# Eight instead of sixteen taps of a 31-tap depthwise convolution on TensorE, the rest on VectorE

## The chip, the cores and the metric

The kernel runs on one core of a Trainium2 chip. Its engines work beside each other, each through a queue of its own that is served in order: TensorE (PE, its weight loads PEld), VectorE (DVE), ScalarE (ACT), GpSimd (POOL) and SyncE (SP), which here only issues DMA transfers. The metric is the time of one execution on the device in microseconds (us). The kernel before takes 2657.86 us (median of 3 runs, 2657.32 to 2660.58).

## The reference

One inference step of a two-layer diffusion backbone over 128 prompt tokens and 512 latent tokens, 640 in all, with 1024 channels in float32. Each layer is a gated feed-forward part, a mixer, and a second feed-forward part, each with a residual. The mixer of the second (odd) layer is the one that matters here:

```python
def gmlp_conv_mixer(h, w_in, v_ln_g, v_ln_b, sp_w, sp_b, dw_w, dw_b, cn_g, cn_b, w_out):
    u, v, ga, gg = jnp.split(h @ w_in, [D_C, 2 * D_C, 2 * D_C + D_D], axis=-1)
    u = jax.nn.gelu(u)
    v = layer_norm(jax.nn.gelu(v), v_ln_g, v_ln_b)
    vc = v.reshape(b, L // MLP_CHUNK, MLP_CHUNK, N_HEADS_C, HEAD_DIM_C)
    sv = jnp.einsum('hts,bcshd->bcthd', sp_w, vc) + sp_b.T[None, None, :, :, None]
    y_c = u * sv.reshape(b, L, D_C)
    glu = ga * jax.nn.sigmoid(gg)
    y_d = jax.nn.silu(layer_norm(depthwise_conv_centred(glu, dw_w, dw_b), cn_g, cn_b))
    return jnp.concatenate([y_c, y_d], axis=-1) @ w_out
```

`depthwise_conv_centred(glu, dw_w, dw_b)` convolves each of the 1024 channels of `glu` along the tokens with 31 taps of its own (`CONV_D = 31`), the 128 and the 512 tokens apart, and adds a bias.

## The kernel before

**Layout.** Activations are stored with channels on the 128 partitions and tokens along the free dimension: eight blocks of 128 channels by 640 tokens. The tokens are worked on in two halves of 320, A and B. A dense product in float32 is made of three products of rounded parts (`mm3`: high weight times high input, high times low, low times high), so that each weight block arrives by DMA (`wr`, issued by SP, L206), is cast to its high part on ACT (`wh`, L216), and has its low part taken on DVE (`wl`, L217). The prefetch runs two weight units ahead, and four raw buffers hold what has landed and is not yet split.

**The odd mixer, in the order of TensorE.** First the `ga` and `gg` products for the eight channel blocks j (each 48 matmuls for half A, then 48 for half B); their gated product goes into a padded tile `pads[j]` of 685 columns (L1301). Then the `v` products (in two passes q of four weight units each, 512 columns wide, L1333 to L1335). Then the `u` products for eight blocks, each followed, two blocks late, by the spatial product `sv` (L1353), whose result is combined on DVE (L1358, L1360) into `yc[j]`. The eight `yc` are split into high and low parts (L366 on ACT, L367 on DVE). Then come 16 tasks `ooc` (the output product over the `yc`), with the layer norm of the convolution woven in, and last the output product over the normalized convolution, `ood`.

**The convolution of a block j** has 31 taps. `PE_TAPS` of them run on TensorE, as matmuls on 32 x 32 diagonal blocks: `rep_next` copies the padded tile four times by 16 DMAs on the SP queue, each copy shifted by one more token (`rep`, L1254), and builds the diagonal weights on DVE (`diag`, L1257); `conv` then runs four matmuls for each group of four taps and each of two column halves (L1269), and ACT brings the sum with the bias into a tile `cacc` of 655 columns (L1272). The other taps are a chain on DVE: each step multiplies the padded tile, shifted by one token, with the tap's weight and adds it to `cacc` in place (L1276); the last tap writes the result `co[j]` (L1281, two pieces). So a step of one chain needs the step before it, while steps of two blocks' chains do not need each other.

```python
ng = PE_TAPS // 4
dg = ph.tile([P, ng * 4, 32], F32, tag="s", name=nm("diag"))
...
for m in range(PE_TAPS // 4):
    for q in range(4):
        TE.matmul(ps[32 * q:32 * q + 32, :q1 - q0], lhsT=dg[:, 4 * m + q, :],
                  rhs=R[q][:, 4 * m + q0:4 * m + q1], ...)
S.activation(out=ac[:, q0:q1], in_=ps[:, :q1 - q0], func=AF.Identity, bias=cvc("dw_b", j))
rep_next()
with tc.high_priority(offset=-CONV_LATE):
    for i in range(PE_TAPS, CONV_D - 1):
        V.scalar_tensor_tensor(out=ac, in0=pad[:, i:i + 655], ..., in1=ac, ...)
```

**What sets the order.** TensorE's order is written out by hand: block j's convolution runs at the slots `CONV_AT = (1, 2, 3, 4, 5, 7, 9, 11)`, five between the A and B halves of the gate products and three between the units of the `v` products. `LN_STEPS` puts the sums of the layer norm over all eight `co[j]` (`ln_sum`, L1389, 32 matmul records) directly before the first `ooc` task. The other engines' order is fixed ahead of the run by a planner: on each engine it takes, among the instructions that it holds ready at that moment of its own plan, the one of highest priority, and an instruction that is not ready in the plan is passed over. The taps on DVE have the lowest priority (`CONV_LATE = 3000`), so all else that is ready goes first. On the chip each engine then keeps that order. Padded tiles, `rep`, `diag`, `cacc`, `co`, `yc` and some others share one pool of 21 buffers (`OB`).

Of the kernel before, what the change touches and what calls it, by code (L numbers as in the profile page):

```python
# [30 lines left out]
RB = 4  # L31
NSTD = 3
TAP_EARLY = 400
PE_TAPS = 16
RW = 655 + PE_TAPS - 4
REPS = 1
OB = 21
# [34 lines left out]
def build(tc, ap):  # L72
# [3 lines left out]
    with ctx:  # L76
# [11 lines left out]
        def nm(p):  # L88
            uid[0] += 1
            return f"{p}_{uid[0]}"  # L90
# [49 lines left out]
        def psum(cols=512):  # L140
            return pspool.tile([P, cols], F32, tag="ps", name=nm("ps"))
# [13 lines left out]
        def cvc(name, i):  # L155
            o = CV[name] + i
            return cv[:, o:o + 1]
# [1062 lines left out]
        def odd(prev):  # L1220
# [26 lines left out]
            def rep_next():  # L1247
# [4 lines left out]
                for r in range(4):  # L1252
                    for q in range(4):
                        nc.sync.dma_start(out=R[q][32 * r:32 * r + 32, :], in_=pads[j][32 * q:32 * q + 32, r:r + RW])  # L1254
                ng = PE_TAPS // 4
                dg = ph.tile([P, ng * 4, 32], F32, tag="s", name=nm("diag"))
# [4 lines left out]
            def conv(j):  # L1261
# [3 lines left out]
                for q0, q1 in ((0, 328), (328, 655)):  # L1265
                    ps = psum()
# [3 lines that stand above are left out]
                                      rhs=R[q][:, 4 * m + q0:4 * m + q1],  # L1270
                                      start=(m == 0), stop=(m == PE_TAPS // 4 - 1))
# [4 lines that stand above are left out]
                        V.scalar_tensor_tensor(out=ac, in0=pad[:, i:i + 655], scalar=cvc("dw_w", i * 8 + j), in1=ac,  # L1276
# [285 lines left out]
```

## Time and profile before

| What | Value |
|---|---|
| Median of 3 runs | 2657.86 us |
| The profiled execution, its own time | 2652.47 us |
| Its span in the trace | 2650.7 us |
| Mean granted TensorE clock over the span | 0.987 of full speed |
| The odd mixer's first convolution on PE starts at | 1842.1 us in the span |
| ScalarE (ACT) busy from 1842.70 to 2064.00 | 59.30 us |

Times in the trace count from the span's start. An engine's busy time says how long it worked, not whether anything waited for it. TensorE's matmuls are pipelined: a record's duration is longer than the step from one start to the next, so the rate is read from starts, or from the pieces of the chain that ended last. Idle time of an engine is followed by the engine and line that released it. Profile and timed runs are different executions.

### The profile page before, as it was taken

How to read it: one execution, taken by the hardware profiler on the slowest of the kernel's cores; microseconds unless marked ns; L12 is line 12 of the kernel's file. 1: busy time of each engine (PE TensorE's matmuls, PEld its weight loads, DVE VectorE, ACT ScalarE, POOL GpSimd, SP SyncE). 2: the span in 40 equal slices, each digit the busy share in tenths (PEclk: the TensorE clock that was granted, in tenths of full speed). 3: DMA queues.
4: the chain of work that ended last, by engine and by line, in shares of the span. 5: the costliest groups of instructions: out<-in, count | busy, mean ns of one | idle time of the engine just before them, and what ended most of it. 6: DMA issues, size and time to landing. Idle time of an engine off the chain costs nothing. (4 is left out here: it accounts for less than half of the span.)

```text
span 2650.7 us, 43732 instructions
## 1 busy us (share of the span) xinstructions
PE 2525.2 (95%) x17229; PEld 2434.1 (92%) x17229; DVE 1936.4 (73%) x3265; ACT 1245.7 (47%) x2316; POOL 154.4 (6%) x255
## 2 busy tenths in 40 slices
PE   7899999899999999999999999989999999999997
PEld 5899999889989999999999999989879998999997
DVE  6778878589986977677597777855985749554465
ACT  4444445458863644445354444543223536444552
POOL 0011110000000010101001011000000000101100
PEclk9999999999999999999999999999999999999999
DMA  7487876222112376767238687724431123656641
GB/s 283 122 225 205 214 220 168 76 70 64 48 53 88 104 207 182 204 187 196 80 116 212 182 227 210 198 93 123 133 112 64 56 72 112 175 143 147 157 120 58
DMA packets 140078, 378.09 MB, mean 143 GB/s; under 512 B 17504, under 2 KB 24160, under 8 KB 139360
## 3 DMA queue, kind: packets, MB, share of 16 engines
q1 hardware_dynamic: 111568, 296.33, 34.4%
q0 software_dynamic: 24768, 71.31, 15.2%
q10 hardware_dynamic: 3536, 7.66, 0.9%
q8 instruction: 135, 2.21, 0.3%
q14 instruction: 71, 0.58, 0.1%
HBM read 329.17 MB, written 3.67 MB: 126 GB/s over the span
## 5 line engine op out<-in xcount | busy, mean ns | idle before, releaser
L217 DVE TENSOR_TENSOR wl<-wr,wh 128x1024 fp32r<-128x1024 f32 (+3 forms) x393 | 390.6, 997 | 294.4 <-ACT wh L216 107.3
L216 ACT CAST wh<-wr 128x1024 fp32r<-128x1024 f32 (+3 forms) x393 | 339.7, 868 | 376.8 <-DMA wr<-in_wd 119.2
L384 PE MATMUL ps<-h,wl 128*128 128x320 f32 x1408 | 436.9, 310 | 9.8 <-DVE wl L217 9.8
L382 PE MATMUL ps<-h,wh 128*128 128x320 f32 x1408 | 437.0, 310 | 6.3 <-ACT h L366 6.3
L383 PE MATMUL ps<-h,wh 128*128 128x320 f32 x1408 | 436.1, 310 | 3.1 <-DVE h L367 3.1
L745 PE MATMUL ps<-quad,wh 128*128 128x320 f32 x1824 | 406.8, 311 | 3.8 <-ACT tmp L727 3.8
L745 PE MATMUL ps<-th,wh 128*128 128x320 f32 x1216 | 382.3, 314 | 28.4 <-ACT tmp L727 22.9
L745 PE MATMUL ps<-th,wl 128*128 128x320 f32 x1216 | 380.0, 313 | 3.6 <-DVE wl L217 3.6
L745 PE MATMUL ps<-tl,wh 128*128 128x320 f32 x1216 | 379.3, 312 | 0.0
L313 DVE CUSTOM_DVE_ANT_0 junk<-wm,crow,cv 128x1024 bf16<-128x1024 f32 x256 | 327.6, 1280 | 3.3 <-DMA wm<-in_wm 0.7
L382 PE MATMUL ps<-pair,wh 128*128 128x320 f32 (+1 forms) x976 | 309.3, 317 | 8.4 <-ACT pair L375 5.8
L745 PEld LDWEIGHTS ps<-quad,wh 128*128 128x128 f32 x1824 | 307.7, 189 | 4.6 <-ACT tmp L727 4.5
L383 PE MATMUL ps<-pair,wh 128*128 128x320 f32 (+1 forms) x976 | 304.0, 312 | 2.1 <-DVE pair L377 2.1
L384 PE MATMUL ps<-pair,wl 128*128 128x320 f32 (+1 forms) x976 | 303.7, 311 | 0.0
L745 PE MATMUL ps<-quad,wl 128*128 128x320 f32 x912 | 283.5, 311 | 4.9 <-DVE wl L217 4.9
L384 PEld LDWEIGHTS ps<-h,wl 128*128 128x128 f32 x1408 | 264.6, 188 | 14.0 <-DVE wl L217 14.0
L382 PEld LDWEIGHTS ps<-h,wh 128*128 128x128 f32 x1408 | 264.6, 188 | 8.3 <-ACT h L366 8.0
L383 PEld LDWEIGHTS ps<-h,wh 128*128 128x128 f32 x1408 | 264.6, 188 | 5.2 <-DVE h L367 4.7
L745 PEld LDWEIGHTS ps<-th,wh 128*128 128x128 f32 x1216 | 231.4, 190 | 35.4 <-ACT tmp L727 28.4
L217 DVE TENSOR_TENSOR wl<-ws,wh 128x1024 fp32r<-128x1024 f32 x152 | 185.3, 1222 | 92.0 <-ACT wh L216 37.0
L745 PEld LDWEIGHTS ps<-th,wl 128*128 128x128 f32 x1216 | 231.5, 190 | 4.9 <-DVE wl L217 4.9
L745 PEld LDWEIGHTS ps<-tl,wh 128*128 128x128 f32 x1216 | 231.5, 190 | 0.0
(262 smaller groups left out, 4398.1 us busy)
## 6 DMA issues: line engine op xcount, KB each, us to landing
wm<-in_wm SPq DMA_DIRECT2D x128, 512.0 KB, 4.4
wr<-in_wgu SPq DMA_DIRECT2D x76, 512.0 KB, 4.7
ws<-in_wgu SPq DMA_DIRECT2D x152, 256.0 KB, 3.9
ws<-in_wgu POOLq DMA_DIRECT2D x76, 512.0 KB, 6.8
x<-y POOLq DMA_DIRECT2D x96, 320.0 KB, 5.8
wr<-in_wd SPq DMA_DIRECT2D x64, 384.0 KB, 3.5
wr<-in_wd SPq DMA_DIRECT2D x64, 320.0 KB, 3.5
wr<-in_wgu SPq DMA_DIRECT2D x76, 256.0 KB, 3.8
```

Source lines behind the costliest of these rows:

```text
L216: S.copy(hi, src)
L217: state["paced"] = V.tensor_sub(lo, src, hi).ins
L313: V.tensor_tensor_reduce(out=junk[0], in0=w, in1=crow[cond], scale=1.0, scalar=cvc("b_mod", L * 72 + idx * KC + c), op0=ALU.mult, op1=ALU.add,
L382: TE.matmul(ps, lhsT=wh, rhs=xh, start=start, stop=False)
L383: TE.matmul(ps, lhsT=wh, rhs=xl, start=False, stop=False)
L384: TE.matmul(ps, lhsT=wl, rhs=xh, start=False, stop=stop)
L745: TE.matmul(ps[:, :TH], lhsT=l[k], rhs=r[:, k, :], start=(first and k == 0 and n == 0), stop=(k == 3 and n == 2), skip_group_check=True)
```

## The change

`PE_TAPS` becomes 8. With it the loop over `m` has two steps instead of four, the diagonal weights have 256 columns instead of 512, the shifted copies are `RW` = 659 instead of 667 columns wide, and the chain on DVE starts at tap 8 instead of tap 16: 22 steps of L1276 and the last tap, instead of 14 and the last tap.

```diff
--- before.py
+++ after.py
@@ -31,7 +31,7 @@
 RB = 4
 NSTD = 3
 TAP_EARLY = 400
-PE_TAPS = 16
+PE_TAPS = 8
 RW = 655 + PE_TAPS - 4
 REPS = 1
 OB = 21
```

## Rows read from the trace of the kernel before

**Rows 1.** The page, busy us (share of the span) and instructions of each engine.

```profile
PE 2525.2 (95%) x17229; PEld 2434.1 (92%) x17229; DVE 1936.4 (73%) x3265; ACT 1245.7 (47%) x2316; POOL 154.4 (6%) x255
```

**Rows 2.** Busy time by stretch: PE, PEld, DVE, ACT, POOL, clock, DMA, GB/s.

```profile
1842.70:2064.00 221.30, 221.30 (x1642) 189.07 (x1635) 170.96 (x233) 59.30 (x87) 0.58 (x9) 1.00 0.36 105
1845.20:2071.46 226.26, 225.70 (x1666) 192.95 (x1659) 176.64 (x243) 61.52 (x91) 0.58 (x9) 1.00 0.35 101
```

**Rows 3.** The chain that ended last: start us, us, what.

```profile
1842.14 4.54 PE ps L1269 x64
...
1860.96 4.54 PE ps L1269 x64
...
1981.26 4.54 PE ps L1269 x64
...
2064.87 2.29 PE ps L1389 x32
...
2067.72 1.32 PE ps L1397 x4
2069.04 0.14 PE ps L382
2069.18 0.15 PE ps L383
```

**Rows 4.** DVE idle in the u stage, and its end: start us, us, what.

```profile
2028.83 1.23 DVE L217 TENSOR_TENSOR wl<-wr,wh 128x1024 fp32r<-128x1024 f32 x1 [5.20 <-issue]
...
2068.13 2.28 DVE L367 TENSOR_TENSOR pair<-slab,pair 128x640 fp32r<-128x640 f32 x3
2070.33 1.21 DVE L217 TENSOR_TENSOR wl<-wr,wh 128x1024 fp32r<-128x1024 f32 x1
```

**Rows 5.** Groups on DVE, 1840 to 2072: xcount | busy, mean ns | idle before.

```profile
L1276 DVE SCALAR_TENSOR_TENSOR cacc<-pad,cv,cacc 128x655 f32<-128x655 f32 x112 | 100.8, 900 | 15.4 <-ACT cacc L1272 9.4 <-issue 3.2
L1257 DVE TENSOR_TENSOR diag<-id,cw 128x512 f32<-128x512 f32 x7 | 4.8, 684 | 0.0
L1360 DVE TENSOR_TENSOR slab<-slab,tmp 128x256 f32<-128x256 f32 x8 | 3.3, 416 | 0.0
```

**Rows 6.** Busy by stretch of L1276 alone, then of L1281 alone: DVE, clock, DMA.

```profile
1845.20:2071.46 226.26, 100.78 (x112) 1.00 0.35 101
...
1845.20:2071.46 226.26, 8.52 (x16) 1.00 0.35 101
```

**Rows 7.** DVE by time around the first chain of taps.

```profile
1847.40 0.90 DVE L1276 SCALAR_TENSOR_TENSOR cacc<-pad,cv,cacc 128x655 f32<-128x655 f32 x1 [2.54 <-ACT cacc L1272]
1848.21 0.68 DVE L1257 TENSOR_TENSOR diag<-id,cw 128x512 f32<-128x512 f32 x1
...
1855.96 7.46 DVE L1276 SCALAR_TENSOR_TENSOR cacc<-pad,cv,cacc 128x655 f32<-128x655 f32 x8
...
1866.26 1.84 DVE L1276 SCALAR_TENSOR_TENSOR cacc<-pad,cv,cacc 128x655 f32<-128x655 f32 x2 [1.33 <-ACT cacc L1272]
```

**Rows 8.** DVE by time in the even mixer, taps of its 5-tap convolution (L840).

```profile
667.29 0.89 DVE L840 SCALAR_TENSOR_TENSOR cacc<-pad,cv,cacc 128x642 f32<-128x642 f32 x1
668.09 0.61 DVE L1157 SCALAR_TENSOR_TENSOR slab<-slab,cv,ps 128x384 f32<-128x384 f32 x1
```

**Rows 9.** Busy by stretch around a stop of PE before the odd mixer.

```profile
1788.00:1795.00 7.00, 5.69 (x20) 5.35 (x21) 7.00 (x23) 4.09 (x11) 0.00 (x0) 0.51 0.77 297
1795.00:1800.00 5.00, 5.00 (x34) 4.84 (x33) 5.00 (x13) 2.73 (x7) 0.00 (x0) 1.00 0.01 3
```

**Rows 10.** PE by time at the same stop.

```profile
1788.33 0.63 PE L382 MATMUL ps<-pair,wh 128*128 128x320 f32 x1 [2.32 <-ACT pair L375]
1789.94 0.64 PE L383 MATMUL ps<-pair,wh 128*128 128x320 f32 x1 [0.98 <-DVE pair L377]
```

**Rows 11.** SP by time: the copies for the fifth convolution.

```profile
1893.75 10.81 SPq L1254 DMA_DIRECT2D rep<-pad  x16
```

**Rows 12.** Waits of the SP queue, 1840 to 2010: us in total, times, longest.

```profile
SPq L206 <- DVE wl L217: 85.5, 18, 9.7
```

## The prediction

> **What bounds the kernel now.** I read the page's busy line first: TensorE works for 95% of the span and VectorE for 73% [rows 1]. That average says little about the one stage that changes, so I next asked for busy time from the first convolution on PE to the sums of the layer norm: there PE never stops (221.30 of 221.30 us), at full clock, while DVE works 170.96 us [rows 2]. Third, the chain that ended last runs over PE through that stage, and every one of the eight convolutions stands in it with 4.54 us [rows 3] (the first two and the last of the eight stand there). So before the change PE is the bound of the stage, and DVE has 226.26 - 176.64 = 49.6 us of idle time between 1845.20 and 2071.46 [rows 2]. Part of it lies in the u stage, where DVE waits 5.20 us before a weight split because it has nothing else [rows 4]; before the first step of a chain it also waits, 2.54 or 1.33 us, for the block's PE part [rows 7], so a chain is finished before the next one can begin.
>
> **What is removed.** A convolution is 64 matmul records in 4.54 us [rows 3], and half of them go: 2.27 us each, 8 x 2.27 = 18.2 us of PE, all on the path. Left to itself PE would reach the layer norm's sums at 2064.87 - 18.2 = 2046.7 instead of 2064.87 [rows 3]. No row shows a convolution of half the size; if a fixed part did not shrink, PE would gain less than 18.2 us, down to nothing, but the sum below hangs on DVE and not on this. Building the diagonal weights shrinks from 128x512 to 128x256. The nearest row for that is another tensor-tensor of 128x256, 416 ns against 684 [rows 5], so 7 x 0.27 = 1.9 us leave DVE in the stage. The copies keep their 16 DMAs per block and lose 8 of 667 columns; I count nothing for it.
>
> **What is added.** 8 blocks x 8 taps = 64 more steps of L1276 on DVE, to the 112 that are there [rows 5]. What one costs depends on its neighbour. In a row of eight steps of one chain, each needing the one before, 7.46 us pass [rows 7]: (7.46 - 0.90) / 7 = 0.937 us from start to start. Where an instruction that doesn't need it follows, it starts after 0.81 us (1847.40 to 1848.21) [rows 7]. In the even mixer the planner puts other work between the steps of a chain wherever some is ready, and there a step takes 0.80 us (667.29 to 668.09) although it lasts 0.89 [rows 8]. Once two blocks' chains are waiting, I expect the same of them: steps of the two in turn, at 0.81 us each.
>
> **Do two chains wait?** A gate period on PE takes 18.82 us before (1842.14 to 1860.96 [rows 3]), 16.55 us after. A block will need 22 steps, 17.8 us at 0.81, and 8.52 / 8 = 1.07 us for its last tap [rows 6], and other DVE work (two weight splits, the gate products, the diagonal) of about 3.5 us: a period of 18.86 us from chain to chain less a wait of 1.33 [rows 7], less 14 steps at 0.92 and 1.07. That is 22.4 us of work in 16.55 us: a backlog from the first block on, growing by about 6 us a block. It is worked off in the u stage, where DVE was half idle. So DVE has work without a gap from about 1845.2 (the first chain can start some 2.3 us earlier than 1847.40 [rows 7]).
>
> **The sum on DVE.** Its work from 1845.20 to 2071.46, to the last split of `yc` and one weight split behind it [rows 2, 4], is 176.64 us. Less the old taps, 100.78 and 8.52 [rows 6], 67.3 us remain; less 1.9 for the diagonals, 65.5. To this come 8.52 for the last taps and 176 steps:
> all at 0.81: 142.6, sum 216.6, end at 2061.8;
> all at 0.937: 164.9, sum 238.9, end at 2084.1.
> I take 40 steps at 0.937 (some 15 of the first block while it is alone, some 10 of the second, the second half of the last) and 136 at 0.81: 147.6, sum 221.7, end at 2066.9. This is the nearer end because the even mixer's rows show the planner doing it. The planner's order is unknown; gaps that it leaves on DVE would add to this.
>
> **What it means for PE.** PE is at the sums at 2046.7 and DVE is done at about 2067, so some 20 us of PE must be waiting somewhere: at once before the sums, or in pieces earlier, behind late weight splits or gate products. Nothing of the 18.2 us is left over. When the `ooc` task can start depends on what DVE does last:
> (a) The taps last. Of the 32 sum records 17 are left when the last `co` comes, 1.2 us at the rate of 2.29 / 32; from the sums' end to the first `ooc` matmul it is 2069.04 - (2064.87 + 2.29) = 1.9 us [rows 3]. Start at 2070.0, 1.0 us later than before.
> (b) The `yc` splits last. The first task needs the eighth `yc` at its 22nd matmul, 21 x 0.15 = 3.1 us after its start [rows 3], so it can start at 2063.8, 5.2 us earlier.
> From there on PE is again the bound and the rest runs as before.
>
> **The clock.** Where PE stops for 2.32 and 0.98 us just before the odd mixer [rows 10], the granted clock is 0.51 (the 1.2 GHz level) over 1788 to 1795 and 1.00 (2.4 GHz) in the next 5 us [rows 9]: 7.0 x 0.49 = 3.4 us lost. A stop of some 20 us before the sums should cost the same 3.4 us once; if the waiting is spread in small pieces, nothing. No row shows a longer stop than that.
>
> So (a) gives +4.4 us and (b) -1.8 us. Which it is the profile doesn't tell; taps have the lowest priority, which speaks for (a), and I take +3 us. The profiled execution takes 2652.47 us (span 2650.7 and 1.8 around it) and would become 2655.5. It lies 5.4 us below the median of the three runs, so I add the difference to the median: 2657.86 + 3, or 2661 us.
>
> **Other waits, costed at nothing.** The copies are issued on the SP queue behind the weight loads, and those wait for DVE's weight splits, 9.7 us at the longest [rows 12]. For the fifth convolution the 16 issues end at 1904.6 [rows 11], some 13 us before it starts on PE (1842.14 + 4 x 18.82 = 1917.4). A late DVE eats into this, and TensorE may stop for some us behind a copy. The pool of 21 buffers gets tight as well: by my count 21 are in use at the fifth convolution (6 padded tiles, 3 `cacc`, 2 `co`, 10 for two sets of copies). What hides both is PE's own 20 us of waiting; they cost time only beyond that, or where they leave DVE without work.
>
> **Rivals.**
> 1. Slower: the chains don't interleave. The mechanism is the order on DVE: each block's chain runs to its end in steps of 0.937 us before the next begins, and the stage ends at 2084.1. With (a) and the clock, 2084.1 + 3.1 + 3.4 - 2069.0 = +21.6 us: 2679.5. For it: before the change all chains run this way; but there only one is ready at a time [rows 7]. Against it: rows 8. It decides from about 48 lone steps on (0.127 us each, with (a) and the clock), where the time passes the 0.2% mark. The Trainium skill's page "VectorE: DVE Perf Modes", section "The DRAIN you can't avoid", speaks for it: an instruction can't start until the pipe of the one before is empty, and leaving semaphores out between instructions saved nothing. By that rule a neighbour that doesn't depend would save nothing and the time would be that of this rival, 2679.5; the trace has 0.81 against 0.937 us, so I go by the trace. Chance 0.2, the stretch between the forecast and it taken in.
> 2. Faster: interleaving is nearly complete, order (b) holds, and PE's waiting comes in pieces, so that the clock stays up. End at 2061.8, `ooc` at 2058.7: -10.3 us, 2647.5. For it: the splits of `yc` can't start before the last `sv`, and end last in the trace before [rows 4]. Against it: it needs all three. Chance 0.13 of passing the 0.2% mark.
> 3. The change doesn't do what it says: PE keeps the 18.2 us because DVE keeps up. That needs DVE to finish by 2046.7, 201.5 us after 1845.2, against at least 216.6. The rows exclude it but for an error of 15 us in them. Chance 0.02, time 2657.9 - 18.2 = 2639.7.
>
> **How the numbers follow.** Forecast, DVE takes PE's place as the bound of this stage and the time hardly moves: 0.65, with its own range of 2654 to 2668. Rival 1 0.2, rivals 2 and 3 0.15. About 0.2%, 5.3 us, is what a measurement of this kernel can tell from no change, that is 2652.5 to 2663.2. Of the forecast's 0.65 I put 0.46 inside and 0.19 above; rival 1 is above but for 0.01. So faster 0.15, same 0.47, slower 0.38. The range reaches to both rivals: 2650 to 2677.
>
> **What would show it.** Right: 32 matmul records in 2.2 to 2.4 us per convolution; 176 steps of L1276, most of them in turn with another block's, at 0.81 us; DVE without a gap of over 1 us from 1846 to about 2065; a wait of PE for a tap of L1281 or L1276 before L1389, or smaller ones before it, of 15 to 22 us together; a granted clock below 1 behind it. Wrong: steps of one chain in long rows (rival 1), or PE without a wait up to the sums (rival 3), or gaps on DVE while taps are left.

## The result and the profile after

The changed kernel takes 2700.47 us (median of 3 runs, 2699.29 to 2704.58) against 2657.86: a ratio of 1.0163, interval 1.0147 to 1.018, or 42.6 us slower. The forecast was 2661.0, its range ended at 2677, and the slower rival stood at 2679.5: the time lies beyond all of them. The profiled execution is the one of 2700.47 us, 48.0 longer than that of before.

The page's busy line now, against [rows 1]; PE is busy for about the same time, and VectorE has 53.9 us more:

```profile
PE 2527.6 (94%) x16973; PEld 2441.5 (90%) x16973; DVE 1990.3 (74%) x3329; ACT 1244.3 (46%) x2316; POOL 154.5 (6%) x255
```

The same stretch as in [rows 2], from the first convolution on PE to the layer norm's sums ("the stage" from here on), and then cut within 0.3 us of the end of the last tap (2068.17). The columns are start and end, length, busy time of PE, PEld, DVE, ACT and POOL, granted clock, DMA share, GB/s:

```profile
1852.20:2112.50 260.30, 216.74 (x1398) 189.69 (x1397) 226.62 (x299) 58.69 (x88) 0.58 (x9) 0.91 0.32 90
...
1852.20:2067.90 215.70, 172.13 (x1089) 145.21 (x1089) 207.63 (x266) 47.45 (x69) 0.58 (x9) 0.90 0.34 96
2067.90:2112.50 44.60, 44.60 (x311) 44.48 (x309) 18.99 (x34) 11.24 (x19) 0.00 (x0) 0.96 0.18 60
```

Before, the stage was 222.7 us without a stop of PE; now it is 260.3. That is 37.6 of the 48.0 us.

```profile
1842.10:2064.80 222.70, 222.70 (x1653) 190.06 (x1653) 171.76 (x235) 59.77 (x88) 0.58 (x9) 1.00 0.36 104
```

Another 10.1 passed ahead of the stage, in code that the change doesn't touch (its first convolution starts at 1852.2 instead of 1842.1). In the runs below that start lies anywhere from 1837.1 to 1852.2, so I count it as the spread of executions and compare stages.

The cut shows the shape of the loss. While there are taps, VectorE is busy for 207.6 of 215.7 us, and PE stands still for 43.6. Then the taps are over, PE still has 44.6 us of the u stage (the `u` products and their `sv`) before it, and VectorE is idle for 25.6 of them. PE's stops, by what ended them (total, times, longest):

```profile
PE ps L1269 <- DMA rep<-pad: 17.7, 2, 13.1
PE ps L382 <- DVE tmp L1358: 13.3, 1, 13.3
PE ps L1269 <- issue: 9.1, 1, 9.1
PE ps L1269 <- DVE diag L1257: 3.5, 1, 3.5
```

All but the second stand at convolutions, ahead of the u stage; the second stands early in it. "Issue" names no releaser, but the trace has one that fits: the stop of 9.1 us ends 0.1 us after the diagonal of that convolution is finished on VectorE (2013.24 + 0.42 = 2013.66), just as the stop of 3.5 us does (1987.81 and 1987.91).

```profile
1987.39 0.42 DVE L1257 TENSOR_TENSOR diag<-id,cw 128x256 f32<-128x256 f32 x1
2013.24 0.42 DVE L1257 TENSOR_TENSOR diag<-id,cw 128x256 f32<-128x256 f32 x1
...
1987.91 2.90 PE L1269 MATMUL ps<-rep,diag 128*32 128x328 f32 x32 [3.47 <-DVE diag L1257]
2013.76 4.20 PE L1269 MATMUL ps<-rep,diag 128*32 128x328 f32 x32 [9.12 <-issue]
```

So 25.9 us of the stops are behind a result of VectorE itself (13.3 for the first `sv` product's combination, L1358, and 12.6 for diagonals), and 17.7 behind copies. VectorE by time, rows of the first three chains, against [rows 7]:

```profile
1863.41 12.20 DVE L1276 SCALAR_TENSOR_TENSOR cacc<-pad,cv,cacc 128x655 f32<-128x655 f32 x13
1875.52 1.22 DVE L217 TENSOR_TENSOR wl<-wr,wh 128x1024 fp32r<-128x1024 f32 x1
...
1884.55 19.69 DVE L1276 SCALAR_TENSOR_TENSOR cacc<-pad,cv,cacc 128x655 f32<-128x655 f32 x21
...
1910.29 17.81 DVE L1276 SCALAR_TENSOR_TENSOR cacc<-pad,cv,cacc 128x655 f32<-128x655 f32 x19
1928.02 1.22 DVE L217 TENSOR_TENSOR wl<-wr,wh 128x1024 fp32r<-128x1024 f32 x1
```

The groups of the stage, against [rows 5] (count, busy us, mean ns, idle before): a step lasts what it lasted, 900 ns, and VectorE hardly waits for anything before one.

```profile
L1276 DVE SCALAR_TENSOR_TENSOR cacc<-pad,cv,cacc 128x655 f32<-128x655 f32 x176 | 158.3, 900 | 5.5
...
L1257 DVE TENSOR_TENSOR diag<-id,cw 128x256 f32<-128x256 f32 x7 | 2.9, 417 | 0.0
```

In the rows by time a chain runs whole: 21 steps in 19.69 us, (19.69 - 0.90) / 20 = 0.94 us a step. Weight splits (L217) stand in the queue behind such rows. What that does to the SP queue, against [rows 11], where the two weight loads ahead of the copies held SP for 4.12 us (the first line here is of before, the others of after):

```profile
1889.54 4.12 SPq L206 DMA_DIRECT2D wr<-in_wov  x2
...
1857.51 22.47 SPq L206 DMA_DIRECT2D wr<-in_woi  x5
1880.41 10.01 SPq L1254 DMA_DIRECT2D rep<-pad  x16
...
1906.94 22.65 SPq L206 DMA_DIRECT2D wr<-in_wov  x3
1929.70 10.03 SPq L1254 DMA_DIRECT2D rep<-pad  x16
```

The weight loads of the second stretch hold SP from 1906.94 to 1929.59; VectorE's split at 1928.02 comes after 19 taps. Only then are the next 16 copies issued, until 1939.73, and PE, in order, waits for them:

```profile
1890.09 5.39 PE L1269 MATMUL ps<-rep,diag 128*32 128x328 f32 x32 [4.62 <-DMA rep<-pad]
1909.68 2.41 PE L1269 MATMUL ps<-rep,diag 128*32 128x328 f32 x32
1939.44 6.26 PE L1269 MATMUL ps<-rep,diag 128*32 128x328 f32 x32 [13.07 <-DMA rep<-pad]
```

The waits of the SP queue over the 170 us that answer to [rows 12] went from 85.5 to 108.4, the longest from 9.7 to 18.9:

```profile
SPq L206 <- DVE wl L217: 108.4, 14, 18.9
```

### The profile page after: what moved, and what is told of

It reads as the page before. It is cut to its first block, busy times and chain, and to the rows that moved or that the text cites. A ratio compares the mean times of both kernels' runs of the same rounds, so it can differ in the third digit from the quotient of the medians.

```text
span 2698.7 us, 43286 instructions
## 1 busy us (share of the span) xinstructions
PE 2527.6 (94%) x16973; PEld 2441.5 (90%) x16973; DVE 1990.3 (74%) x3329; ACT 1244.3 (46%) x2316; POOL 154.5 (6%) x255
## 3 DMA queue, kind: packets, MB, share of 16 engines
q0 software_dynamic: 24768, 71.31, 15.1%
## 5 line engine op out<-in xcount | busy, mean ns | idle before, releaser
L217 DVE TENSOR_TENSOR wl<-wr,wh 128x1024 fp32r<-128x1024 f32 (+3 forms) x393 | 390.3, 996 | 292.2 <-ACT wh L216 115.0
L382 PE MATMUL ps<-pair,wh 128*128 128x320 f32 (+1 forms) x976 | 311.5, 319 | 21.7 <-DVE tmp L1358 13.3
L217 DVE TENSOR_TENSOR wl<-ws,wh 128x1024 fp32r<-128x1024 f32 x152 | 185.3, 1221 | 90.8 <-ACT wh L216 41.8
```

What stands on the lines that cost most here:

```text
L217: state["paced"] = V.tensor_sub(lo, src, hi).ins
L382: TE.matmul(ps, lhsT=wh, rhs=xh, start=start, stop=False)
```

## The experiments

Eight taps and no stop would be a stage of 207.0 us (first run below), so each stage is that, plus PE's stops, plus what PE was busy beyond 207.0 (222.7 for sixteen taps, 214.9 half-way for twelve). In the changed kernel 8.9 of the 9.7 us of that last term are the lower clock behind stops (worked out further down); for the other runs it is not taken apart. Stages, stops and busy times are each of one traced execution. The ratio is to runs of before on the same chip, whose median lay between 2650.64 and 2655.87 beside the runs e1 to e17.

| kernel | time, us | ratio (interval) | stage | stops | beyond | DVE busy |
|---|---|---|---|---|---|---|
| before | 2657.86 | 1 | 222.7 | 0 | 0 | 171.8 |
| changed | 2700.47 | 1.0163 (1.0147-1.018) | 260.3 | 43.6 | 9.7 | 226.6 |
| e1, PE's part alone (taps 8 to 15 left out) | 2642.03 | 0.9947 (0.9928-0.9966) | 207.0 | 0 | 0 | 169.4 |
| e2, VectorE's part alone (taps 8 to 15 twice) | 2681.39 | 1.01 (1.0071-1.013) | 250.5 | 20.7 | 7.1 | 228.8 |
| e3, copies on GpSimd's queue | 2696.86 | 1.0153 (1.0127-1.018) | 265.9 | 44.4 | 14.5 | 225.7 |
| e3b, copies on ScalarE's queue | 2683.63 | 1.0122 (1.0107-1.0137) | 251.0 | 28.9 | 15.1 | 225.5 |
| e6, two sets of copies | 2685.67 | 1.0131 (1.0115-1.0148) | 252.9 | 32.1 | 13.8 | 227.4 |
| e4, convolutions spread | 2674.61 | 1.0073 (1.0051-1.0095) | 244.4 | 30.6 | 6.8 | 226.3 |
| e7, two sums in turn | 2662.73 | 1.0033 (1.0013-1.0052) | 234.1 | 18.1 | 9.0 | 217.7 |
| e8, spread and two sums | 2663.72 | 1.0043 (1.0028-1.0058) | 230.1 | 19.2 | 4.0 | 218.2 |
| e15, two sums, ScalarE's queue | 2679.34 | 1.008 (1.0053-1.0106) | 243.1 | 22.7 | 13.4 | 217.7 |
| e17, two sums, two sets | 2676.48 | 1.0074 (1.0049-1.0099) | 242.4 | 26.7 | 8.8 | 220.2 |
| e11, splits on GpSimd | 2709.44 | 1.0218 (1.0203-1.0233) | 274.1 | 51.4 | 15.8 | 246.2 |
| e12, the same, two sums | 2696.74 | 1.0168 (1.0153-1.0183) | 260.7 | 37.5 | 16.2 | 234.2 |
| e5, twelve taps on PE | 2658.24 | 1.0016 (1.0002-1.0031) | 226.2 | 6.3 | 5.1 | 198.7 |
| e9, twelve, two sums | 2652.46 | 0.9991 (0.9975-1.0008) | 220.0 | 3.3 | 1.8 | 194.2 |
| e13, e9 with ScalarE's queue | 2660.49 | 1.0016 (1.0001-1.003) | 226.1 | 4.7 | 6.5 | 192.9 |
| e16, e9 with two sets | 2658.62 | 1.0015 (0.9999-1.0032) | 229.5 | 9.4 | 5.2 | 197.0 |

**Each half of the change alone (e1, e2).**

```diff
 e1, on the changed kernel
-                    for i in range(PE_TAPS, CONV_D - 1):
+                    for i in range(16, CONV_D - 1):
 e2, on the kernel before
-                    for i in range(PE_TAPS, CONV_D - 1):
+                    for i in range(8, CONV_D - 1):
```

> The changed kernel, but VectorE begins its chain at tap 16, as before the change; taps 8 to 15 are computed nowhere, so the output is not the reference's. TensorE has the half-size convolutions, VectorE the old number of taps. Theory (the added VectorE work is what costs: it holds up copies, weight splits and diagonals, and these stop TensorE ahead of the u stage): with the old VectorE load TensorE runs through, the stage is 222.7 - 18.2 = 204.5 us and the time 2657.9 - 18.2, about 2640 us. Rival (half-size convolutions are themselves bad for TensorE, because the copies have less time to land or the stops drop the clock): the time stays at or above the 2657.9 of before.

> The kernel before, all 16 taps on TensorE, but VectorE's chain begins at tap 8: taps 8 to 15 are counted twice, so the output is not the reference's. TensorE keeps its full load, VectorE has that of the changed kernel. Theory (the added VectorE work alone sets the stage): at least as slow as the changed kernel's 2700.5, with VectorE near 100% from the first chain to the last; 2690 to 2715 us, and TensorE's stops about 18 us shorter than in the changed kernel, since its own work fills them. Rival (the loss needs a TensorE that comes earlier to its stops): with TensorE 18.2 us longer, half of the added VectorE work is hidden and the time is 2660 to 2680 us.

e1 came as its theory had it: ratio 0.9947, and PE doesn't stop. The convolutions on its chain (start, us, what), and its stage in the columns of before:

```profile
1845.71 2.34 PE ps L1269 x32
...
1953.29 2.34 PE ps L1269 x32
1969.47 4.07 PE ps L1269 x32
```

```profile
1845.60:2052.60 207.00, 207.00 (x1400) 182.15 (x1400) 169.36 (x235) 58.42 (x88) 0.58 (x9) 1.00 0.40 112
```

So PE's saving is real: 7 x (4.54 - 2.34) and 0.47 at the last, 15.9 us, and the stage is 15.7 shorter. From e1 to the changed kernel only 64 steps on VectorE are added, and the stage grows by 53.3 us: nearly as much as those steps last (64 x 0.94 = 60 us), although e1's idle VectorE, 37.6 us, could have hidden more than half of them. e2 fell between its two expectations: VectorE's part alone costs 27.8 us of stage, and PE stops for 20.7. What neither expected: the changed kernel's stage is 10 us longer than e2's, though PE has less to do. The taps end at about the same place (218 us after the first convolution in e2, 216 in the changed kernel), but PE then has 32.1 us of the stage left in e2 and 44.6 in the changed kernel. Why it is further on in e2 is not shown; the order of VectorE's queue, planned anew for every kernel, differs, and in e2 no convolution waits for copies:

```profile
PE ps L1269 <- DVE diag L1257: 8.4, 1, 8.4
PE ps L1269 <- issue: 7.5, 2, 5.9
PE ps L1333 <- DVE pad L1301: 4.5, 1, 4.5
```

Both stops put down to "issue" again end 0.1 us after the convolution's diagonal on VectorE, so in e2 PE waits for VectorE in all but 0.3 of its 20.7 us.

**The copies' place (e3, e3b, e6).**

```diff
-                        nc.sync.dma_start(out=R[q][32 * r:32 * r + 32, :], in_=pads[j][32 * q:32 * q + 32, r:r + RW])
+                        nc.gpsimd.dma_start(out=R[q][32 * r:32 * r + 32, :], in_=pads[j][32 * q:32 * q + 32, r:r + RW])
 e3b: nc.scalar.dma_start in its place
 e6, copies left on SyncE
-REPS = 1
+REPS = 2
```

> The changed kernel with the 16 copies of a block issued on GpSimd's DMA queue instead of SyncE's, where they stood behind weight loads. Theory A (VectorE's load is the cause; the late copies are only where it shows): TensorE's 17.7 us of waiting for copies go, and the same time appears as waiting for other VectorE results (splits, diagonals, the products before the u stage); 2690 to 2702 us. Theory B (the copies' place in the SyncE queue is the cause): the 17.7 us come off and with them the low clock behind each stop, 2675 to 2683 us.

> The changed kernel with the copies issued on ScalarE's DMA queue. Unlike GpSimd, ScalarE issues without work of its own per descriptor, so this is the cleaner form of the same question. Theory A (VectorE's load is the cause): waits for copies are replaced by others, 2690 to 2702 us. Theory B (the place in the SyncE queue is the cause): 2675 to 2683 us.

> The changed kernel with two sets of copies ahead instead of one. Theory A (late copies are only where VectorE's load shows): 2690 to 2705 us; two more sets of four buffers are held, and the pool of 21 may add stops of its own. Theory B (copies issued a block earlier land in time): the 17.7 us of waits for copies go, 2675 to 2685 us.

On GpSimd's queue nothing is gained, as theory A had it: the waits for copies go from 17.7 to 2.7 us, and PE stops for 44.4 us all the same, now for other results of VectorE (the four stops put down to "issue" each end 0.1 us after a diagonal):

```profile
PE ps L1269 <- issue: 22.7, 4, 8.0
PE ps L382 <- DVE tmp L1358: 12.9, 1, 12.9
PE ps L1333 <- DVE pad L1301: 6.3, 1, 6.3
PE ps L1269 <- DMA rep<-pad: 2.7, 2, 2.5
```

On ScalarE's queue, and with two sets ahead, the time falls to 2683.63 and 2685.67, at the edge of what the copies' theory expected. In e6 no stop of over 0.3 us at a convolution is left; PE waits for weight splits and for the products of the u stage instead (11.7 and 11.3 us). In e3b waits for the copies shrink to 4.8 us, and a wait put down to taps takes their place (three stops at convolutions, 20.9 us in all). For e3b:

```profile
PE ps L1269 <- DVE cacc L1276: 20.9, 3, 8.3
PE ps L1269 <- DMA rep<-pad: 4.8, 3, 2.2
```

e3b is not a clean test: the copies now hold up ScalarE's own work, and ScalarE is idle behind them for 108.5 us of the stage.

**Where the backlog lies, and what a step costs (e4, e7, e8).**

```diff
 e4
-CONV_AT = (1, 2, 3, 4, 5, 7, 9, 11)
+CONV_AT = (1, 2, 4, 6, 9, 12, 14, 16)
 e7
+                    a2 = ph.tile([P, 655], F32, tag="s", name=nm("cac2"))
                     for i in range(PE_TAPS, CONV_D - 1):
-                        V.scalar_tensor_tensor(out=ac, in0=pad[:, i:i + 655], scalar=cvc("dw_w", i * 8 + j), in1=ac,
+                        if i == PE_TAPS + 1:
+                            V.tensor_scalar(out=a2, in0=pad[:, i:i + 655], scalar1=cvc("dw_w", i * 8 + j),
+                                            scalar2=None, op0=ALU.mult)
+                            continue
+                        t = a2 if (i - PE_TAPS) % 2 else ac
+                        V.scalar_tensor_tensor(out=t, in0=pad[:, i:i + 655], scalar=cvc("dw_w", i * 8 + j), in1=t,
                                                op0=ALU.mult, op1=ALU.add)
+                    V.tensor_add(ac, ac, a2)
 e8: both
```

> The changed kernel with the eight convolutions placed later and wider apart: at the slots 1, 2, 4, 6, 9, 12, 14, 16 instead of 1, 2, 3, 4, 5, 7, 9, 11, so that the last two stand in the u stage. The work is the same. Theory A (VectorE's backlog was piled up ahead of the u stage and stopped TensorE there, while VectorE was half idle in the u stage): the taps now lie beside the u stage as well, TensorE's stops of 43.6 us shrink, and the time is 2655 to 2680 us. Theory B (the sum of VectorE's work is the bound wherever it lies): about 2700 us as before, with the taps ending later and the wait moved ahead of the layer norm's sums.

> The changed kernel with each block's chain on VectorE as two sums in turn (even taps onto the TensorE part, odd taps into a second buffer), and one addition of the two ahead of the last tap. Neighbouring steps then don't need each other. Theory A (a step costs 0.81 us beside an independent neighbour, as the trace of before had it, against 0.937 in a lone chain): 20 of 22 steps save 0.127 us, less an addition of about 0.7 us, 8 x 1.84 = 15 us off VectorE, and the time falls by 10 to 25 us, to 2675 to 2690 us. Theory B (an independent neighbour saves nothing): VectorE has 8 additions more, 2700 to 2708 us.

> Both of these at once on eight taps: convolutions at the slots 1, 2, 4, 6, 9, 12, 14, 16, and two sums in turn. If the backlog ahead of the u stage and the lone steps are the two causes of the loss, this takes away both: VectorE's work about 212 us against 209.7 of TensorE, with stops of 5 to 20 us: 2645 to 2665 us. If VectorE's order in the queue (splits behind rows of taps) is what is left, as late as the run with convolutions spread alone: 2670 to 2675 us.

e4 has the changed kernel's work on VectorE (299 instructions, 226.3 us) and a stage 15.9 us shorter, with the time in theory A's range: where the work lies matters, not its sum alone. After the last tap PE now has 18.7 us left instead of 44.6:

```profile
2066.60:2085.30 18.70, 18.70 (x137) 18.61 (x135) 11.91 (x22) 5.82 (x10) 0.00 (x0) 0.99 0.17 57
```

e7 is the strongest single edit, more than its theory allowed: 26.2 us of stage. VectorE by time in one of its chains:

```profile
1874.55 0.90 DVE L1282 SCALAR_TENSOR_TENSOR cac<-pad,cv,cac 128x655 f32<-128x655 f32 x1
1875.37 0.89 DVE L1282 SCALAR_TENSOR_TENSOR cacc<-pad,cv,cacc 128x655 f32<-128x655 f32 x1
1876.18 0.90 DVE L1282 SCALAR_TENSOR_TENSOR cac<-pad,cv,cac 128x655 f32<-128x655 f32 x1
1876.99 0.90 DVE L1282 SCALAR_TENSOR_TENSOR cacc<-pad,cv,cacc 128x655 f32<-128x655 f32 x1
```

The durations are those of before, 0.9 us, but the starts are 0.81 apart: steps that don't need each other overlap. VectorE's busy time falls by only 8.9 us (an addition of 0.84 and a first product of 0.55 a block are in it), yet the taps end 200.6 us after the first convolution instead of 216.0, and the stops fall from 43.6 to 18.1. Waits for copies are 0.6 us of these: with the steps closer together, the copies come in time although nothing was done to them. e8 adds the spread to it and gains 4.0 us of stage more, which the times don't show (ratio 1.0043 against 1.0033); its time is within the first of its two ranges.

**The copies again, without the lone steps (e15, e17).** e7 with the edits of e3b and of e6.

> Eight taps on TensorE, two sums in turn, copies on ScalarE's DMA queue. Two sums left 18.1 us of stops (diagonal 6.8, issue 5.6, gate product 4.2) and 9.0 us of clock. If late copies are a cause beside the lone steps, the stage falls from 234.1 to 220 to 228 us and the time to that of before or up to 5 us below it; if the copies were late only because the lone steps held up the splits, it stays at 232 to 236 us, some 9 us above before.

> Eight taps, two sums in turn, two sets of copies ahead. As with the copies on ScalarE's queue: 220 to 228 us of stage if late copies are a cause of their own, 232 to 236 us if not, and above that if the eight copy buffers and the second sum use up the pool.

Both are slower than e7, by 9.0 and 8.3 us of stage, and above both ranges of stage (e17's last case, the pool of buffers, is not excluded). They test less than they were meant to, since e7 waits for copies only 0.6 us: there was next to nothing to gain. In e15 PE waits for the copies on ScalarE's queue for 17.1 us; in e17 it waits for none, but for splits and products instead. It is shown, then, that getting the copies out of SP's queue, or issuing them earlier, is no remedy by itself. It is not shown that they cost nothing in the changed kernel: the same two edits take 9.3 and 7.4 us off its stage and add 9.0 and 8.3 to e7's, and each of them changes the whole planned order with the copies.

**The splits off VectorE (e11, e12).**

```diff
-            state["paced"] = V.tensor_sub(lo, src, hi).ins
+            state["paced"] = (G if state.get("pool_split") else V).tensor_sub(lo, src, hi).ins
```

with `pool_split` set from the gate to the end of the u stage's blocks.

> The changed kernel with the low half of each weight split (128x1024, 1.22 us on VectorE) computed on GpSimd from the odd mixer's gate to its u stage. Some 28 splits, 34 us, leave VectorE, and no split stands behind a row of taps any more. Theory A (VectorE's queue is the cause: its load, and the splits and so the weight loads and copies held behind rows of taps): VectorE has some 193 us left beside TensorE's 207, the copies' waits go, and the time is 2642 to 2665 us. Theory B (the splits' place is harmless and only the taps' end counts): 2670 to 2690 us. What no row shows is GpSimd's price of such a split; above 7.4 us each (207 / 28) it would itself be the bound, and the time above 2700 us.

> Two sums in turn and the low halves of the splits on GpSimd, eight taps on TensorE. VectorE has about 226.6 - 15 - 34 = 178 us beside TensorE's 207. If VectorE is then off the path, TensorE runs through and the whole of the 15.7 us that the run with the old VectorE load showed is kept: 2638 to 2648 us, faster than both kernels. If GpSimd slows VectorE or is late itself: 2655 to 2675 us.

Both theories failed, and so does the test: e11 is slower than the changed kernel, e12 slower than either of its ranges, because the edit slows VectorE itself. The groups of e11 over its stage (count, busy us, mean ns, idle before):

```profile
L1277 DVE SCALAR_TENSOR_TENSOR cacc<-pad,cv,cacc 128x655 f32<-128x655 f32 x176 | 196.7, 1118 | 8.1 <-issue 2.2
L217 POOL TENSOR_TENSOR wl<-wr,wh 128x1024 fp32r<-128x1024 f32 x25 | 67.0, 2683 | 197.5 <-PE ps L384 103.0 <-PE ps L1336 73.6 <-ACT wh L216 20.0
```

A split on GpSimd takes 2.68 us, far below the 7.4 that would have made it the bound, but the mean tap goes from 900 to 1118 ns: 176 x 0.218 = 38 us, more than the 25 splits had cost VectorE (30.5 us). So these two runs say nothing on whether the splits' place in VectorE's queue is a cause; that stays argued, from the rows by time.

**Twelve taps (e5, e9, e13, e16).** `PE_TAPS = 12` in the changed kernel (e5), in e7 (e9), and e9 with the edits of e3b and e6.

> Twelve of the 31 taps on TensorE, nineteen on VectorE: between the two kernels. TensorE loses half of what the eight-tap convolutions took away (15.7 / 2 = 7.9 us by the run with the old VectorE load), VectorE gets 32 more steps at 0.937, 30 us, on 171.8 us of work in a stage that then has 217.5. Theory (what decides is whether VectorE keeps up block by block, some 16.5 to 17.5 us of TensorE work each): a block's work on VectorE is 18 steps at 0.937, 1.07 and some 3.5, 21.4 us, still above a gate period of 17.7 us, so the backlog grows only 4 us a block and is gone by the u stage; stops of 0 to 10 us, time 2648 to 2660 us. Rival (any backlog ahead of the u stage costs in proportion to the added taps): half of the 42.6 us, 2679 us.

> Twelve taps on TensorE and VectorE's nineteen as two sums in turn: 18 steps at about 0.81 and one addition. By the theory that two sums save 0.127 us a step, VectorE needs some 8 x (16 x 0.127 - 0.7) = 11 us less than with twelve taps in one chain, about 190 us in a stage of 217.5, TensorE never stops, and the time is that of before less 7.9 us: 2646 to 2652 us. If an independent neighbour saves nothing it is that of twelve taps in one chain or 5 us above it.

> Twelve taps on TensorE, two sums in turn on VectorE, and the copies issued on ScalarE's DMA queue. With twelve taps and two sums TensorE stopped once, 3.3 us for a copy, and the stage took 220.0 us; half-way between 222.7 and 207.0 is 214.9. If that stop and the low clock behind it are due to the copies' place behind weight loads, the stage is 215 us and the time that of before less 7 us, some 2646 to 2652 us; if the copies hold up ScalarE's own work, or the stop moves elsewhere, it stays within 4 us of before.

> Twelve taps, two sums in turn, two sets of copies ahead on the SyncE queue. The other way to have the copies earlier: if the one stop of 3.3 us goes, the stage is 215 us and the time 7 us below before; if the pool of 21 buffers stops TensorE instead, at before or up to 10 us above it.

With twelve taps the loss is nearly gone (not half of it, as the proportional rival had it), but the expected gain doesn't come either: e5 stops for 6.3 us and is busy 5.1 beyond its due, which is more than the 7.8 us saved. e9 has the shortest stage of any version that computes all the taps, 220.0 us, and the lowest time, 0.9991 of before, which its interval (0.9975 to 1.0008) doesn't tell from no change; its time, 2652.46, is at the upper edge of its range. The copies' edits made it longer again (e13 ends above both of its cases, e16 in the worse of its two). No version that computes the whole convolution beat the kernel before.

## Why the prediction was wrong

**Right: what bounds before and the parts.** PE was the bound; half-size convolutions take 2.34 us (2.27 forecast), and left to itself PE's stage is 15.7 us shorter (18.2 forecast; in e1 the eighth convolution takes 4.07 us at full clock, and its weight loads wait in it, 0.9 us for copies that are still landing and 1.0 us with no releaser shown). 176 steps, 900 ns each, 0.94 apart in a lone chain, and VectorE without a gap while taps are left: all as written.

**Wrong, step "Do two chains wait? ... steps of the two in turn, at 0.81 us each".** The backlog was there from the first block, but VectorE's queue never takes two chains in turn: rows of 13, 21 and 19 steps of one chain. That is rival 1's mechanism, given 0.2. [rows 8] was no evidence for it: there other work stands between the taps of a chain, not a second chain. The prediction told only half of what the Trainium skill's page "VectorE: DVE Perf Modes" states in the section "The DRAIN you can't avoid": an instruction starts only when the pipe of the one before is empty, but one that is not held starts earlier. The trace agrees with the second half: e7's independent steps start 0.81 us apart and last 0.9. So the price of 0.81 was right, and the order in which it would be had was not. What the step is worth: with it made true by hand (e7) the time is 2662.7, a ratio of 1.0033, where before took 2654.96; the forecast was 2661 to 2657.86, 1.0012.

**Wrong, step "It is worked off in the u stage", and with it "some 20 us of PE must be waiting somewhere".** The forecast, and rival 1, took VectorE's sum as the end of the stage and left open where PE waits. But the place decides. PE's stops came ahead of the u stage and at its beginning, so that the u stage, the one place where VectorE had time to spare, moved behind the taps. The stretch of the forecast's sum on VectorE, from its start (1855.06 here, 1845.20 before) to the weight split behind the last `yc` split:

```profile
1855.06:2119.24 264.18, 220.06 (x1418) 192.70 (x1417) 232.80 (x309) 60.53 (x91) 0.39 (x6) 0.91 0.30 87
```

The work itself is what the upper sum had: 238.9 us with all steps at 0.937, of which 176 x 0.037 = 6.5 are gaps between steps, leaves 232.4 busy; measured are 232.8. The stretch takes 264.2 us where the forecast had 221.7, 42.5 more. Of these, 17.2 are the steps' price (238.9 - 221.7, rival 1), and the other 25.3 are idle time behind the last tap (25.6 us by the window in the section on the result), where VectorE waits for PE to go through the u stage. The sum had it at nothing. PE's stops are 43.6 us, where the prediction had some 20. e4, which moves the last convolutions into the u stage, is the test of this: same work, 15.9 us less.

**Wrong, "Other waits, costed at nothing".** It named the copies behind weight loads and held that PE's own waiting hides them. It was these waits (17.7 us), together with those for diagonals (12.6) and for the first `sv` product's combination (13.3), that PE's waiting consisted of. They were not hidden: each of them put off the u stage, or what was left of it. Whether the copies add something of their own stays open (above).

**Mis-sized, "The clock": 3.4 us once.** There was a stop at five places, and behind four of them the granted clock is low (behind the stop of 3.5 us it stays at 1.00):

```profile
1890.00:1895.50 5.50, 5.41 (x33) 2.04 (x33) 5.22 (x7) 0.53 (x1) 0.00 (x0) 0.62 0.76 209
...
1939.40:1945.60 6.20, 6.16 (x32) 2.14 (x32) 5.88 (x8) 0.53 (x1) 0.00 (x0) 0.52 0.73 189
2013.70:2017.90 4.20, 4.14 (x33) 3.64 (x33) 4.06 (x5) 0.53 (x1) 0.00 (x0) 0.60 0.33 115
...
2065.50:2072.00 6.50, 4.70 (x18) 4.70 (x19) 4.08 (x8) 0.00 (x0) 0.00 (x0) 0.52 0.24 81
```

PE's busy time in each, times the share of the clock that is missing, is 5.41 x 0.38 + 6.16 x 0.48 + 4.14 x 0.40 + 4.70 x 0.48 = 8.9 us. In all PE is busy 9.7 us longer than in e1 for the same work. The convolution at 0.52, near the 1.2 GHz level, takes 6.26 us where one at full clock takes 2.41 (both in the rows by time above). That is more than the clock makes of it (2.41 / 0.52 = 4.6 us); SP issues the last of its copies only after it has begun (1939.73 against 1939.44), which may be the rest.

**In sum.** 260.3 = 207.0 + 43.6 of stops + 9.7 in which PE is busy longer, mostly by the clock. The cause that the runs show is VectorE's load, which alone turns 207.0 into 260.3 (e1 against the changed kernel). Of these 53.3 us two sums gave back 26.2, another place for the convolutions 15.9, and both together 30.2. VectorE's busy time, 226.6 us, is longer than the whole stage of before: with its steps in lone chains this change could not have gained, even without a gap on VectorE. What stays open is why the planner puts rows of up to 21 taps between two weight splits, what the late copies add of their own, and the 5 us by which the medians differ more than the stages.

## What to carry to other kernels

When a move makes another engine the bound of a stretch, its sum of work is only the lower end: ask where the engine that used to be the bound will stop, and whether that stop pushes away the very stage in which the new bound was to catch up. In queues fixed ahead, a long row of low-priority work is a wait for everything behind it, and for the queues that wait for that. And a long chain of dependent steps on VectorE was better written as two sums in turn, with eight taps on TensorE (e7) and with twelve (e9).

## What the hardware showed that I had not expected

Two 128x655 multiply-adds on VectorE that don't depend on each other start 0.81 us apart, though each lasts 0.9; dependent ones 0.94.

A subtraction on GpSimd holds up VectorE's taps. In e11, by time on VectorE and on GpSimd:

```profile
1913.00 19.09 DVE L1277 SCALAR_TENSOR_TENSOR cacc<-pad,cv,cacc 128x655 f32<-128x655 f32 x16
```

```profile
1917.57 2.42 POOL L217 TENSOR_TENSOR wl<-wr,wh 128x1024 fp32r<-128x1024 f32 x1 [20.15 <-PE ps L384]
1921.08 2.81 POOL L217 TENSOR_TENSOR wl<-wr,wh 128x1024 fp32r<-128x1024 f32 x1 [1.10 <-PE ps L384]
```

Sixteen steps should take 15 x 0.94 + 0.90 = 15.0 us and take 19.1; in the row lie 5.2 us of GpSimd's subtractions, so VectorE loses 4.1 of them. The Trainium skill's page "GPSIMD Engine Reference", section "Key points", says that GpSimd shares its SBUF interfaces with VectorE and that they contend where VectorE has two SBUF inputs; a tap has two, and the trace agrees: the 141 taps of e11 with no such subtraction beside them last 900 ns on average, as before, and the 35 that overlap one 2.0 us, up to 3.1.

The subtractions are held up too. With VectorE idle beside them they last 2.4 us, in e11 up to 3.1; in e12, beside steps that start 0.81 us apart, six of 28 last 4.5 to 10.5 us (spans on GpSimd are rough in the profile):

```profile
1869.18 9.81 POOL L217 TENSOR_TENSOR wl<-wr,wh 128x1024 fp32r<-128x1024 f32 x1 [9.04 <-ACT wh L216]
```
